# Two heads at a time in a dilated attention, and four more tiles for expert weights, in a two-block kernel on one core

## The chip, the core and the metric

The kernel runs on one core of a Trainium2 chip. The core has a matrix engine (PE in the profile, with its weight loads as PEld), a vector engine (DVE), an activation engine (ACT), a general engine (POOL) and a queue engine that issues transfers (SP). The metric is the device time of one execution in microseconds (us); smaller is better.

## What is computed

The program is a diffusion-style block of two layers, and then a second block of another kind, on 256 tokens of width 1024, batch 1, all in float32. The change lies in the second block alone, whose reference is, cut to what matters:

```python
def dilated_branch(q, k, v, window, dilation):   # query i sees keys i + j*dilation, |j| <= window // (2*dilation)
    ...
    s = jnp.where(valid, q @ k.T * 64 ** -0.5, -inf)
    m = max(s); p = exp(s - m); return p @ v, m, sum(p)
...
for window, dilation in ((128, 1), (512, 4), (2048, 16)):      # 12 heads of 64
    num, den, m = merged over the three branches
...
def second_block(x, mem, ...):
    u = rms_norm_2(x) @ w_in                                   # conv part, q, k, v
    c = conformer_conv(u[..., :512], ...)                      # gate, 31 depthwise taps, layer norm, silu
    a = dilated_attention(q, k, v, positions)
    x = x + concatenate([rms(c), rms(a)]) @ w_out
    x = x + memory_cross_attention(rms(x), rms(mem), ...)
    x = x + hierarchical_moe(rms(x), ...)                      # 32 experts, 2 per token
```

The kernel merges the three branches into one softmax: where a key is seen by n branches, 8 ln n is added to its score before the scale 1/8, and -1e30 where it is seen by none. This table of 256 by 256 is called the mask here.

## The kernel before

All weights are stored in HBM and are read once, in pieces of 128 partitions by 1024 float32 values (512 KB). They and most activations live in one pool of equal tiles in the on-chip memory, `u`, each 4 KB per partition; its size is `NSLOT`, 42 tiles. A transfer into a new tile must wait until the tile that had the place before is no longer read. Small work tiles are `t`, `s`; PSUM tiles are `ps`, eight banks.

Most matrix products use three passes in the fast rounding format fp32r: a weight piece is split by ACT (the high part, `u<-u 128x1024`) and by DVE (the rest, `TENSOR_TENSOR u<-u 128x1024`), then 24 matmuls of 256 columns follow on PE for each piece. Plain float32 matmuls take two records each in the trace.

The order of the work is planned when the program is built. Generators (one for the projections, one for the attention, one for the convolution, ...) yield the data that they wait for next; `drive` steps the one whose data will be there first by a small planner's clock (`Timer`), and pulls a filler, here the values of the later memory attention (weights `w_xv`), when all would wait. The engines then run their queues strictly in that order. `PACE` spaces out the 31 taps of the conformer's convolution, which are VectorE work: tap t is let go when the planner's PE clock has advanced by PACE times (t + 1) us.

The second block runs in these stages, with their place in the trace. From 1354 to 1475 us: the projections (`projections2`, weights w_in), the conformer's convolution (`conformer`) and the dilated attention (`dilated_attention`). From 1475 us: the product with w_out (`project_mix`), whose first matmuls read the conformer's output, the tile pair called Mc here, and then the attention's. From 1512 to 1566 us: memory attention, with weights w_xq and w_xo. Then the routing, and from 1595 us the 32 experts (`moe`), 384 pieces of weights.

Expert pieces are asked for ahead: `pump(n)` issues transfers until n pieces are waiting, and `AHEAD` holds n for six places: the memory attention's queries, the two parts of w_xo, the start of the experts, and two places within them. One piece after the other stands in SP's queue, between the weights of the stage that runs. When the first expert product starts, tiles are held by the pieces, by four tiles of the hidden state, two of the one-hot routing and one scratch tile; three pieces lie in other tiles (`tab`, `t`).

In the attention before, one head is done at a time. Its scores are two plain float32 matmuls that contract over 64 rows, half of the array; behind each, two fp32r matmuls with the identity (`identr`) add the high and the low part of the mask in PSUM. `softmax_pair` takes the maximum on DVE out of PSUM, the exponential on ACT, and the division. `turn_probs` transposes, and two matmuls with 64 output rows give the head's output.

Of the kernel before, what the change touches and what calls it, by code (L numbers as in the profile page):

```python
# [12 lines left out]
F32R = mybir.dt.float32r  # L13
# [3 lines left out]
OP = mybir.AluOpType  # L17
# [13 lines left out]
NSLOT = 42  # L31
# [387 lines left out]
class Net:  # L419
# [3 lines left out]
    PACE = 1.5  # L423
# [8 lines left out]
    AHEAD = (6, 16, 27, 34, 27, 28)  # L432
# [1085 lines left out]
    def start_second(self):  # L1518
# [11 lines left out]
        self.identr = self.cp.tile([128, 128], F32R, name="identr")  # L1530
        nc.scalar.activation(self.identr, self.ident, AF.Copy)
# [69 lines left out]
    def rotary_tables(self):  # L1601
# [6 lines left out]
        ln = self.tmp().rearrange("p (i k) -> p i k", i=2)  # L1608
        nc.gpsimd.dma_start(ln, self.a["lnmult"])
        ang, n, r = (self.tmp()[:, :SEQ] for _ in range(3))  # L1610
        yield (pos, ln)
# [11 lines left out]
        self.mask = Part(self.u([128, 2, 2, SEQ], F32R))  # L1623
        self.divide([(self.mask[:, 0], self.mask[:, 1], ln)], [self.mask])
# [52 lines left out]
    def softmax_pair(self, ps, scale):  # L1677
# [3 lines left out]
        P = Part(self.tmps(SEQ)[0])  # L1681
        nc.vector.tensor_reduce(m, ps, axis=AX, op=OP.max)
# [74 lines left out]
    def dilated_attention(self, Q, K, V, A, then):  # L1757

        nc = self.nc
        P, PT, turned = {}, {}, self.pairs(SEQ)  # L1760
        for hd in range(HEADS2 + 3):
            if hd < HEADS2:
                c, rows = hd // 2, slice(64 * (hd % 2), 64 * (hd % 2) + 64)
                while len(K) <= c:
                    yield BLOCK
                yield from self.until(Q[c], K[c], self.mask)
# [9 lines left out]
            if 0 <= hd - 2 < HEADS2:  # L1776
                yield from self.until(P[hd - 2])
                PT[hd - 2] = self.turn_probs(P.pop(hd - 2), next(turned))
            if hd >= 3:
                g = hd - 3  # L1780
                while len(V) <= g // 4:
                    yield BLOCK
# [620 lines left out]
```

## Time and profile before

| | us |
|---|---|
| median of 3 runs | 2062.21 (2062.17 to 2062.32) |
| the profiled execution | 2062.49 |
| its span in the trace | 2060.7 |
| PE busy over the span | 1935.8 (94%) |
| DVE busy over the span | 1085.6 (53%) |
| ACT busy over the span | 715.9 (35%) |
| expert weights, 384 pieces | 201.3 MB of 432.1 MB |

Shares over the whole span mix stages with different limits, so the stretches are read apart. A busy PE is not PE at its peak, since starts and ends of matmuls overlap: what a matmul costs in a queue is the distance between starts. Times in the rows are counted from the start of the span.

### The profile page before, as it was taken

What the parts mean: (1) busy time and instruction counts of PE and PEld (TensorE: products, weight loads), DVE (VectorE), ACT (ScalarE), POOL (GpSimd) and SP (SyncE); (2) the same over time, 40 slices, a digit from 0 to 9 for tenths busy, and PEclk for the clock granted to TensorE, in tenths of its full rate; (3) what the DMA queues carried; (4) which work ended last, traced back from release to release, by engine and by line L of the source; (5) the groups of instructions that cost most, each with busy time, mean ns of one, the idle gap of its engine ahead of it and who ended that gap; (6) DMA issues with size and microseconds to landing.
All of it is one profiled execution on the core that took longest, in us unless ns stands there. A gap on an engine that the chain in (4) does not pass through costs nothing. (4 is left out here: it accounts for less than half of the span.)

```text
span 2060.7 us, 28054 instructions
## 1 busy us (share of the span) xinstructions
PE 1935.8 (94%) x11179; PEld 1449.0 (70%) x11179; DVE 1085.6 (53%) x1759; ACT 715.9 (35%) x1170; POOL 41.2 (2%) x49
## 2 busy tenths in 40 slices
PE   7999999998999999999999999999999888888886
PEld 3788777886878888899889999998899421111111
DVE  6988888256863333598878655577664210000001
ACT  3433664233332222364654444446652100000001
POOL 0000000000000000000000000000000000000000
PEclk9999999998999999999999999999999999999998
DMA  9533235333543332545267455543269999999997
GB/s 368 168 101 122 67 97 184 124 121 112 169 136 103 92 114 72 166 162 190 68 244 263 158 183 185 176 141 113 92 198 340 395 409 409 409 409 409 409 409 299
DMA packets 121438, 432.11 MB, mean 210 GB/s; under 512 B 13654, under 2 KB 14152, under 8 KB 121304
## 3 DMA queue, kind: packets, MB, share of 16 engines
q1 hardware_dynamic: 119464, 424.64, 57.6%
q0 software_dynamic: 1696, 5.38, 0.9%
q8 instruction: 89, 1.46, 0.3%
q14 instruction: 45, 0.37, 0.1%
q10 hardware_dynamic: 144, 0.26, 0.0%
HBM read 428.13 MB, written 2.10 MB: 209 GB/s over the span
## 5 line engine op out<-in xcount | busy, mean ns | idle before, releaser
L289 PE MATMUL ps<-u 128*128 128x256 f32 (+2 forms) x9088 | 1599.5, 345 | 51.1 <-DVE u L289 24.6
L289 PEld LDWEIGHTS ps<-u 128*128 128x128 f32 (+1 forms) x9088 | 1294.5, 186 | 342.2 <-DMA u<-w 105.8
L289 DVE TENSOR_TENSOR u<-u 128x1024 fp32r<-128x1024 f32 (+4 forms) x414 | 432.6, 1071 | 205.5 <-ACT u L289 166.7
L289 ACT ACTIVATE u<-u 128x1024 fp32r<-128x1024 f32 (+3 forms) x392 | 360.4, 960 | 281.1 <-DVE u L289 224.8
L289 PE MATMUL ps<-u,t 128*32 128x512 f32 (+1 forms) x1028 | 216.9, 620 | 36.0 <-DMA u<-w 21.2
L289 PEld LDWEIGHTS ps<-u,t 128*32 128x32 f32 (+1 forms) x1028 | 44.2, 112 | 192.9 <-DMA u<-w 116.4
L289 ACT ACTIVATE u<-ps 128x512 f32<-128x512 f32 (+3 forms) x207 | 92.2, 487 | 226.9 <-PE ps L289 223.7
L289 DVE TENSOR_TENSOR t<-t,ps 128x512 f32<-128x512 f32 x12 | 8.2, 685 | 259.8 <-PE ps L289 259.8
L289 DVE SCALAR_TENSOR_TENSOR u<-u,cs 128x1024 f32<-128x1024 f32 x112 | 140.1, 1278 | 0.8 <-DMA u<-w_mod 0.7
L289 ACT ACTIVATE t<-ps 128x512 f32<-128x512 f32 (+1 forms) x62 | 36.2, 594 | 266.3 <-PE ps L289 266.2
L289 DVE TENSOR_TENSOR u<-u,ps 128x512 f32<-128x512 f32 x53 | 36.1, 686 | 105.6 <-PE ps L289 105.6
L289 DVE SCALAR_TENSOR_TENSOR u<-ps,mod,u 128x256 f32<-128x256 f32 x96 | 41.9, 479 | 83.4 <-PE ps L289 83.3
L289 DVE SCALAR_TENSOR_TENSOR u<-ps,s,u 128x512 fp32r<-128x512 f32 (+2 forms) x24 | 15.4, 662 | 118.1 <-ACT u L289 98.3
L289 DVE TENSOR_TENSOR u<-ps,u 128x128 fp32r<-128x128 f32 (+2 forms) x135 | 59.9, 490 | 29.2 <-ACT u L289 22.9
L289 ACT ACTIVATE u<-t 128x512 fp32r<-128x512 f32 (+1 forms) x74 | 41.6, 591 | 85.3 <-DVE t L289 76.7
L289 ACT ACTIVATE u<-ps,s 128x512 fp32r<-128x512 f32 (+1 forms) x26 | 15.8, 640 | 154.4 <-PE ps L289 150.8
L289 ACT ACTIVATE t<-ps,s 128x256 f32<-128x256 f32 (+1 forms) x80 | 49.2, 623 | 46.6 <-DVE s L289 45.8
L289 POOL TENSOR_TENSOR s<-s,mhalf 128x4 f32<-128x4 f32 (+2 forms) x25 | 30.0, 1200 | 1676.1 <-DVE s L289 1676.1
L289 PE MATMUL ps<-ident,t 128*128 128x128 f32 (+1 forms) x352 | 49.0, 273 | 7.4 <-DVE t L289 7.3
L289 ACT ACTIVATE t<-u 128x512 f32<-128x512 f32 x41 | 25.3, 628 | 84.9 <-DVE u L289 84.7
L289 PEld LDWEIGHTS ps<-ident,t 128*128 128x128 f32 (+1 forms) x352 | 39.7, 140 | 19.4 <-DVE t L289 14.9
L289 DVE TENSOR_REDUCE s<-ps 128x1 f32<-128x512 f32 (+2 forms) x65 | 38.4, 617 | 17.1 <-PE ps L289 16.9
(130 smaller groups left out, 705.2 us busy)
## 6 DMA issues: line engine op xcount, KB each, us to landing
u<-w SPq DMA_DIRECT2D x381, 512.0 KB, 10.2
u<-w_in SPq DMA_DIRECT2D x102, 512.0 KB, 4.2
u<-w_mod SPq DMA_DIRECT2D x96, 512.0 KB, 4.5
u<-w_gu SPq DMA_DIRECT2D x88, 512.0 KB, 4.0
u<-w_dn SPq DMA_DIRECT2D x32, 512.0 KB, 3.6
u<-w_out SPq DMA_DIRECT2D x24, 512.0 KB, 4.3
u<-w_oa SPq DMA_DIRECT2D x16, 512.0 KB, 4.6
u<-w_dn SPq DMA_DIRECT2D x16, 384.0 KB, 3.2
```

Of the source, the lines that this page charges most:

```text
L289: return fn(*args, **kw)
```

## The change

Six edits, of which the first three belong together.

1. `dilated_attention` takes a pair of heads at a time. The scores of the two heads use rows 0 to 63 and 64 to 127 of the array, in turn, into two PSUM banks; the two heads' outputs go to the two halves of the columns of one bank, in turn, and are copied out together.
2. The two matmuls per score that added the mask are gone, with the identity and the split mask that they read. `softmax_pair` adds the mask on DVE instead, out of PSUM into a work tile, which the maximum and the exponential then read.
3. The transposes of a pair come one step after its scores, where a head's came two steps after.
4. `PACE` goes from 1.5 to 2.2.
5. `NSLOT` goes from 42 to 46, and the six numbers of `AHEAD` go up by 3 or 4.
6. The scratch that POOL's transfers use for their descriptors is set to 2048 bytes per partition, from a default of 16384; the four tiles take the room.

```diff
-NSLOT = 42
+NSLOT = 46
...
-    PACE = 1.5
+    PACE = 2.2
...
-    AHEAD = (6, 16, 27, 34, 27, 28)
+    AHEAD = (9, 19, 30, 38, 31, 32)
...
-        self.identr = self.cp.tile([128, 128], F32R, name="identr")
-        nc.scalar.activation(self.identr, self.ident, AF.Copy)
...
-        ln = self.tmp().rearrange("p (i k) -> p i k", i=2)
-        nc.gpsimd.dma_start(ln, self.a["lnmult"])
+        self.mask = self.u([128, 2, SEQ])
+        nc.gpsimd.dma_start(self.mask, self.a["lnmult"])
...
-        self.mask = Part(self.u([128, 2, 2, SEQ], F32R))
-        self.divide([(self.mask[:, 0], self.mask[:, 1], ln)], [self.mask])
...
-    def softmax_pair(self, ps, scale):
+    def softmax_pair(self, ps, scale, add=None):
...
+        if add is not None:
+            nc.vector.tensor_tensor(P.ap, ps, add, op=OP.add)
+            ps = P.ap
...
-        for hd in range(HEADS2 + 3):
+        n = HEADS2 // 2
+        for c in range(n + 2):
...
-                ps = self.ps().rearrange("p (i k) -> p i k", i=2)
+                ps = [self.ps().rearrange("p (i k) -> p i k", i=2) for _ in range(2)]
                 for i in range(2):
-                    q = slice(i * 128, (i + 1) * 128)
-                    nc.tensor.matmul(ps[:, i], Q[c][rows, q], K[c][rows], start=True, stop=False,
-                                     skip_group_check=True)
-                    for part in range(2):
-                        nc.tensor.matmul(ps[:, i], self.identr, self.mask[:, part, i], start=False, stop=part == 1,
-                                         skip_group_check=True)
-                P[hd] = self.softmax_pair(ps, 0.125)
+                    for hh in range(2):
+                        rows = slice(64 * hh, 64 * hh + 64)
+                        nc.tensor.matmul(ps[hh][:, i], Q[c][rows, i * 128:(i + 1) * 128], K[c][rows], start=True,
+                                         stop=True, skip_group_check=True)
+                P[c] = [self.softmax_pair(p, 0.125, self.mask) for p in ps]
...
                 for k in range(2):
-                    nc.tensor.matmul(ps[:64], v[:, k, cs], pt[:, k], start=k == 0, stop=k == 1)
-                rows = slice(64 * (g % 2), 64 * (g % 2) + 64)
-                nc.scalar.activation(A[g // 4][rows, g // 2 % 2], ps[:64], AF.Copy)
+                    for hh in range(2):
+                        c0 = 64 * (2 * (g % 2) + hh)
+                        nc.tensor.matmul(ps[64 * hh:64 * hh + 64], v[:, k, c0:c0 + 64], pt[hh][:, k], start=k == 0,
+                                         stop=k == 1, skip_group_check=True)
+                nc.scalar.activation(A[g // 2][:, g % 2], ps, AF.Copy)
...
-    nc = bacc.Bacc("TRN2", target_bir_lowering=False, num_devices=1)
+    nc = bacc.Bacc("TRN2", target_bir_lowering=False, num_devices=1, dynamic_dma_scratch_size=2048)
```

PE before, in the middle of the attention, around the scores of the fifth and the sixth head; `u_12811` and `u_12579` hold Q and K, `identr_103` the identity, `64x256` is a head's output:

```order
L289 MATMUL ps_12877<-u_12811,u_12579 128x256
L289 MATMUL ps_12877<-u_4373,identr_103 128x256 x2
L289 MATMUL ps_12877<-u_12811,u_12579 128x256
L289 MATMUL ps_12877<-u_4373,identr_103 128x256 x2
L289 MATMUL ps_12900<-ident_76,t_12540 128x128 x4
L289 MATMUL ps_12906<-u_12602,u_12579 64x256 x2
L289 MATMUL ps_12912<-u_12811,u_12579 128x256
```

PE now, at the scores of the same two heads (third pair of six):

```order
L289 MATMUL ps_12901<-u_12780,u_12491 128x256
L289 MATMUL ps_12902<-u_12780,u_12491 128x256
L289 MATMUL ps_12901<-u_12780,u_12491 128x256
L289 MATMUL ps_12902<-u_12780,u_12491 128x256
L289 MATMUL ps_12933<-ident_76,t_12550 128x128 x4
L289 MATMUL ps_12939<-ident_76,t_12560 128x128 x4
L289 MATMUL ps_12945<-u_12659,u_12491 64x256 x4
```

Four score matmuls of two heads now stand together, with no matmul of the mask between them, and the four output matmuls of an earlier pair stand together too.

DVE now, from the splits of weights behind which that pair's softmax stands to the rotation of the next queries (`t<-ps,u` is the new addition of the mask, the SCALAR_TENSOR_TENSOR rows with `cols` are convolution taps, two per tap):

```order
L289 TENSOR_TENSOR u<-u 128x1024 x3
L289 TENSOR_TENSOR t<-ps,u 128x512
L289 TENSOR_REDUCE s<-t 128x2
L289 TENSOR_SCALAR s<-s 128x2
L289 TENSOR_TENSOR t<-ps,u 128x512
L289 TENSOR_REDUCE s<-t 128x2
L289 TENSOR_SCALAR s<-s 128x2
L289 RECIPROCAL s<-s 128x2
L289 SCALAR_TENSOR_TENSOR t<-u,cols,t 128x256 x4
```

Where one head's maximum stood alone between taps, two heads' additions and maxima now stand in a row, with taps still in the queue, which had run out before this point.

SP at the memory attention, as a piece of the difference; `u<-w` are expert pieces:

```order
 L289 DMA u<-w_xq 128x1024 x8
 L289 DMA u<-w 128x1024 x6
-L289 DMA u<-w_xo 128x1024 x8
+L289 DMA u<-w_xo 128x1024
+L289 DMA u<-w 128x1024 x3
+L289 DMA u<-w_xo 128x1024 x7
 L289 DMA u<-w 128x1024 x15
```

Three more expert pieces now stand ahead of seven of the eight pieces of w_xo.

## Rows read from the trace of the kernel before

**Rows 1.** Stretches: us, busy us of PE, PEld, DVE, ACT, POOL; clock, DMA share, GB/s.

```profile
1354.00:1474.00 120.00, 119.56 (x831) 101.08 (x830) 89.92 (x181) 70.46 (x150) 1.39 (x2) 1.00 0.32 106
...
1595.00:2044.00 449.00, 384.75 (x1777) 98.40 (x1778) 37.21 (x72) 23.23 (x41) 0.58 (x1) 0.98 1.02 405
```

**Rows 2.** Timeline of PE, attention: start, us, what, count of records [idle before].

```profile
1379.46 0.70 PE L289 MATMUL ps<-u 64*128 64x256 f32 x2
1380.08 0.50 PE L289 MATMUL ps<-u,identr 128*128 128x256 f32 x2
1380.51 0.70 PE L289 MATMUL ps<-u 64*128 64x256 f32 x2
...
1468.38 1.08 PE L289 MATMUL ps<-u 128*64 128x256 f32 x4
```

**Rows 3.** Timeline of PE, the first expert product.

```profile
1595.33 3.64 PE L289 MATMUL ps<-u,t 128*32 128x512 f32 x32 [0.58 <-DVE t L289]
```

**Rows 4.** Groups by shape, 1340 to 1505 us: an addition out of PSUM on DVE (us, mean ns).

```profile
L289 DVE TENSOR_TENSOR u<-ps,u 128x512 fp32r<-128x512 f32 x2 | 1.4, 684 | 0.0
```

**Rows 5.** Timeline of DVE in the attention's stretch.

```profile
1361.51 0.69 DVE L289 TENSOR_TENSOR t<-ps,tab 128x512 f32<-128x512 f32 x1 [5.38 <-PE ps L289]
...
1364.35 0.74 DVE L289 TENSOR_SCALAR t<-u,cols 128x256 f32<-128x256 f32 x2
...
1367.74 0.74 DVE L289 STREAM_SHUFFLE t<-ps 128x512 f32<-128x512 f32 x1
...
1370.28 2.46 DVE L289 SCALAR_TENSOR_TENSOR t<-u,cols,t 128x256 f32<-128x256 f32 x6
1372.65 1.22 DVE L289 TENSOR_TENSOR u<-u 128x1024 fp32r<-128x1024 f32 x1
...
1381.79 0.69 DVE L289 TENSOR_REDUCE s<-ps 128x2 f32<-128x512 f32 x1
...
1382.58 0.87 DVE L289 SCALAR_TENSOR_TENSOR t<-u,cols,t 128x256 f32<-128x256 f32 x2
```

**Rows 6.** Timeline of DVE: the conformer's layer norm begins; Mc is finished.

```profile
1423.09 0.69 DVE L289 TENSOR_REDUCE s<-ps 128x2 f32<-128x512 f32 x1 [2.10 <-PE ps L289]
...
1456.19 0.69 DVE L289 TENSOR_TENSOR u<-t,u 128x512 fp32r<-128x512 f32 x1 [1.26 <-ACT u L289]
```

**Rows 7.** Timeline of PE: last head's output, then 36 matmuls with w_out.

```profile
1473.75 5.54 PE L289 MATMUL ps<-u 128*64 128x256 f32 x40
```

**Rows 8.** Timeline of PE, then a stretch as in rows 1, at its end.

```profile
1504.60 1.86 PE L289 MATMUL ps<-ones,t 128*128 128x1 f32 x8 [2.17 <-ACT t L289]
1506.33 5.38 PE L289 MATMUL ps<-u 128*128 128x256 f32 x24
...
1500.00:1510.00 10.00, 7.83 (x46) 7.62 (x46) 8.28 (x15) 5.29 (x8) 2.55 (x5) 0.73 0.90 273
```

**Rows 9.** Timeline of SP: expert pieces (`w`), first issue, us to the last, count.

```profile
1502.46 20.35 SPq L289 DMA_DIRECT2D u<-w  x6
...
1541.71 23.20 SPq L289 DMA_DIRECT2D u<-w  x15
1564.96 0.93 SPq L289 DMA_DIRECT2D tab<-w  x2
...
1568.65 21.15 SPq L289 DMA_DIRECT2D u<-w  x14
...
1597.27 42.66 SPq L289 DMA_DIRECT2D u<-w  x38
```

**Rows 10.** A stretch as in rows 1: where the experts start.

```profile
1590.00:1600.00 10.00, 8.35 (x68) 4.81 (x67) 6.03 (x19) 0.47 (x1) 0.00 (x0) 1.00 0.65 233
```

**Rows 11.** Waits from 1354 to 1480 us: us in total, times, longest.

```profile
DVE s L289 <- PE ps L289: 12.0, 7, 2.7
DVE t L289 <- PE ps L289: 11.1, 4, 5.4
```

**Rows 12.** Transfers issued by POOL: count, KB each, median us to landing.

```profile
stash<-u POOLq DMA_DIRECT2D x4, 256.0 KB, 7.2
```

More of the change, by code (lines that the diff above doesn't have):

```diff
@@ L1760, in dilated_attention @@
         P, PT, turned = {}, {}, self.pairs(SEQ)
-        for hd in range(HEADS2 + 3):
-            if hd < HEADS2:
-                c, rows = hd // 2, slice(64 * (hd % 2), 64 * (hd % 2) + 64)
+        n = HEADS2 // 2
+        for c in range(n + 2):
+            if c < n:
                 while len(K) <= c:
                     yield BLOCK
-                yield from self.until(Q[c], K[c], self.mask)
-                ps = self.ps().rearrange("p (i k) -> p i k", i=2)
+                yield from self.until(Q[c], K[c])
+                ps = [self.ps().rearrange("p (i k) -> p i k", i=2) for _ in range(2)]
@@ L1776, in dilated_attention @@
[L1776 to L1781, printed above, removed]
+                    for hh in range(2):
+                        rows = slice(64 * hh, 64 * hh + 64)
+                        nc.tensor.matmul(ps[hh][:, i], Q[c][rows, i * 128:(i + 1) * 128], K[c][rows], start=True,
+                                         stop=True, skip_group_check=True)
@@ L1782, in dilated_attention @@
+                P[c] = [self.softmax_pair(p, 0.125, self.mask) for p in ps]
+                del ps
+            if 0 <= c - 1 < n:
+                yield from self.until(*P[c - 1])
+                PT[c - 1] = [self.turn_probs(p, next(turned)) for p in P.pop(c - 1)]
+            if c >= 2:
+                g = c - 2
+                while len(V) <= g // 2:
                     yield BLOCK
-                yield from self.until(V[g // 4], PT[g])
+                yield from self.until(V[g // 2], *PT[g])
@@ L1784, in dilated_attention @@
                 pt = PT.pop(g)
-                v = V[g // 4]
+                v = V[g // 2]
                 ps = self.ps()[:, :SEQ]
-                cs = slice(64 * (g % 4), 64 * (g % 4) + 64)
                 for k in range(2):
-                    nc.tensor.matmul(ps[:64], v[:, k, cs], pt[:, k], start=k == 0, stop=k == 1)
-                rows = slice(64 * (g % 2), 64 * (g % 2) + 64)
-                nc.scalar.activation(A[g // 4][rows, g // 2 % 2], ps[:64], AF.Copy)
-                if g % 4 == 3:
-                    then(g // 4)
+                    for hh in range(2):
+                        c0 = 64 * (2 * (g % 2) + hh)
+                        nc.tensor.matmul(ps[64 * hh:64 * hh + 64], v[:, k, c0:c0 + 64], pt[hh][:, k], start=k == 0,
+                                         stop=k == 1, skip_group_check=True)
@@ L1795, in conformer @@
+                nc.scalar.activation(A[g // 2][:, g % 2], ps, AF.Copy)
+                del ps
+                if g % 2:
+                    then(g // 2)
     def conformer(self, C, out):
```

2 lines of the change are left out of this document (1 added, 1 removed).

## The prediction, made before the changed kernel ran

> **What bounds the kernel now.** I read the stretches first, then the queues inside them. In the attention's stretch PE is busy 119.56 of 120 us at a granted clock of 1.00, DVE 89.92, and the DMA share is 0.32 [rows 1]: matmuls set the time, and DVE has 30 us left. From the experts' start at 1595 to 2044 the DMA share is 1.02 at 405 GB/s [rows 1]: there transfers set the time, 449 x 405 = 181.8 MB, or 347 pieces of 524 KB at 1.295 us each. So the change can gain in two ways: less PE time before the experts, or fewer pieces still to load when they start. DVE's waits [rows 11] tell what slack it has today: 23.1 us in waits for PSUM results.
>
> **Scores and outputs on halves (PE).** A half of a head's scores starts at 1379.46, its mask at 1380.08, the next half at 1380.51 [rows 2]: 0.62 + 0.43 = 1.05 us, four times for a pair, 4.2. The mask's 0.43 goes. Of the 0.62, streaming is about 0.45: sixteen float32 matmuls of 512 columns on quarters of the array take 3.64 [rows 3], 0.228 each with four side by side, so 0.91 for one alone and 0.45 for 256 columns; the other 0.17 is changing over. Two halves side by side: 2 x 0.45 + 0.15 = 1.05 a pair. Outputs: four records in 1.08, starts 0.25 apart [rows 2], so 1.0 a head and 2.0 a pair; side by side 1.0. Six pairs give 6 x (3.2 + 1.0) = 25 us. That column quarters overlap, rows 3 show (0.228 against 0.5 for half the columns); that row halves do no row shows, so its bounds are both halves overlapping (25) and neither (4 x 0.45 + 0.1 = 1.9 a pair and outputs unchanged: 14). I take 25, since the pieces of rows 3 are the nearest.
>
> The Trainium skill ("TensorEngine Tiling (Array Packing)", Theoretical Speedup and Gotcha 1) puts row halves at up to twice the speed if they write different PSUM banks, as they do here. No row of before shows it.
>
> **The mask on DVE.** Twelve additions out of PSUM. The same shape has a mean of 684 ns [rows 4]; by starts, less the overhang of some 0.08, 0.60. So 7.2 to 8.2 us more for DVE. Whether this costs nothing depends on where DVE stands, which I count through its queue. Prices, each a duration less about 0.08: a tap (two instructions, 0.87, or 2.46 for three) 0.395 per instruction, a split 1.14 [rows 5]; a rotation of queries or keys 2.54 (three 512-wide products and a shuffle at 0.6 to 0.66 each [rows 5]); a head's softmax 0.60 for the addition and 0.79 for maximum and scale (1381.79 to 1382.58 [rows 5]), 1.40; a division's reciprocal 0.08.
>
> From the first tap, 1364.35 [rows 5], to the end of the fifth pair's key rotation the changed order holds on DVE 54 tap instructions (21.3), 14 splits (16.0), 6 rotations (15.2), eight heads (11.2) and small ones (1.2): 64.9, so 1429.2, and 1431.5 with the waits for PE that I find in the order on the way. PE has up to the same place 444 matmuls of 0.122 (36 in 5.54 less 1.00 for the outputs ahead and an overhang [rows 7]; 54.0), nine groups of transposes (4.0), four pairs of scores (4.2) and two of outputs (2.0): from 1361.4, where DVE's long wait ends [rows 5], that is 64.2, or 1425.6. **So DVE, not PE, is now last there**, by about 6 us, which PE waits. Wider-spread taps are the reason: they stand among the softmaxes.
>
> From there to the first matmul with w_out PE has scores 2.1, transposes 5.0, outputs 4.0, 120 matmuls 14.6, sums with ones and their spreads 4.6: 30.3. Waits in it: for the last taps and the conformer's transposes 2.3, the last pair's softmax 1.3, the conformer's sums 1.6 (each a DVE or ACT step with nothing else ready on PE in the order): 5.5 with small ones. So w_out starts at 1431.5 + 30.3 + 5.5 = 1467.3. Before, it starts at 1473.75 + 1.00 = 1474.75 [rows 7]: 7.4 earlier. As fillers, 24 matmuls with w_xv (2.9), twelve sums and two spreads (3.0), which stood behind that point, now stand ahead of it: 5.9 more. Together 13.3 of the 25; without any wait w_out would start at 1455.9 and all 25 would be kept, which checks the count (1474.75 - 25 + 5.9 = 1455.7).
>
> New waits may also lower the clock. In 1500 to 1510 the granted clock is 0.73, that is partly at 1.2 instead of 2.4 GHz; PE had waited 2.17 for ACT, and the 24 matmuls behind took 5.38 instead of 2.9 [rows 8]: 2.4 for one such fall. I charge one: **11 us** kept.
>
> **Four more tiles, earlier asking.** Before, 6 + 15 + 1 + 2 + 14 = 38 pieces are issued before the first freed tile lets the next go at 1597.27 [rows 9] (the issue pair at 1564.96 is half-size, and with its likes makes three pieces in other tiles); after, 42. Every piece that is there when the experts start shortens their transfers by 1.295: 4 x 1.295 = 5.2. They need room earlier: three stand ahead of w_xo, behind the six issued from 1502.46 on, and 1590 to 1600 has a DMA share of 0.65 [rows 10], 3.5 us unused. Against this the whole span ahead of the experts is shorter, so the fewer idle DMA microseconds cost 0.7: **4.5**. Below: nothing, if SP's queue, in which w_xo's pieces now stand behind three expert pieces (3 x 1.295 = 3.9 later at worst), delays memory attention by as much as the tiles give. At the top 5.2.
>
> **The rest.** A smaller descriptor scratch moves no byte. POOL's four stash transfers take 7.2 to land [rows 12]; if the smaller ring makes POOL stand until one has landed, the routing's small steps behind the last of them on POOL could be up to 7.2 late. A gain is not excluded either (the same transfers from less room), but no row shows POOL waiting for the ring; I take 0 and keep 0 to 7.2. The identity's copy, the mask's split and its load are off the path before the second block; the copies of outputs on ACT become half as many, in a stretch where ACT has 70.46 of 120 [rows 1]. Hidden, and of no cost if they weren't (under 1 us). That transposes follow after one step instead of two shows as the waits above.
>
> **The sum.** 2062.49 (the profiled execution) - 11 - 4.5 = 2047.0; the median is 0.3 below the profiled one, so **2046.7**. About 0.2% (4 us) is what a measurement of this kernel can tell from no change.
>
> **The rivals.**
>
> 1. *PE stays the bound.* DVE starts ahead of its queue and the additions fit the slack of 23.1 [rows 11]; then 25 and 5.2 come in full: 2062.2 - 30 = 2032. For it: 30 us of DVE's stretch are idle. Against: my count of its queue. 0.12.
>
> 2. *Halves don't run side by side.* 11 us of PE's 25 are not there. The waits of 6 us at the fifth pair go first (PE itself is there at 1425.6 + 5.4 = 1431), the other 5.7, behind it, count: 2046.7 + 5 = 2051.7. 0.10.
>
> 3. *The clock falls more often.* With w_out at 1467 and some five waits ahead of it, each may be followed by a slow stretch at 2.4 [rows 8]. Three instead of one: 2046.7 + 4.8 = 2051.5. 0.08. The Trainium skill says as much ("TensorE: Matmul & The Clock Gate", HAM oscillation): gaps between bursts of matmuls can hold the clock at half. Rows 8 agree, with 0.73 behind a gap of 2.17.
>
> 4. *The pieces bring nothing,* since what goes earlier delays w_xo: 2046.7 + 4.5 = 2051.2. 0.05.
>
> 5. *Only the tiles count:* waits for DVE eat all that PE saves: 2062.2 - 4.5 = 2057.7, within what can be told from no change or just beyond. 0.08, which I count as no change.
>
> 6. *Slower: the conformer ends too late.* DVE has its 64.9 us without slack, and taps are spread until 1441 in my count. If it still must wait 23.1 for PE's results as now [rows 11], because it stands in strict order, the last tap comes near 1462.5. From the layer norm's first sum to Mc's low part 33.8 us pass now (1423.09 to 1456.19 + 0.69 [rows 6]), with other work between; then Mc is there at 1496.3, and w_out's first matmuls read it: 21.5 later than 1474.75, less 5.9 moved ahead and 4.5 of tiles: 2062.2 + 11 = 2073. It decides for slower by over 0.2% from Mc at 1489 on, that is 16 of the 23.1. Against it: a third of the chain is other work that would then be done already, and w_xv's matmuls fill. 0.06.
>
> 7. *The change doesn't do what it says:* the ring's size makes POOL wait for a whole landing, 7.2 [rows 12], on top of the forecast: 2053.9. 0.02; nothing in the trace speaks for it.
>
> **How the numbers follow.** The forecast itself has 0.49, with a range of its own from 2040 (DVE gets 6 us ahead of my count) to 2054 (7 more of its waits for PE stay). Faster: 0.49 + 0.12 + 0.10 + 0.08 + 0.05 + 0.02 = 0.86; same 0.08; slower 0.06. For the range, slower and most of the tail of rival 5 stay out above (2058 holds its centre), and below it reaches to rival 1 at 2032: about 0.8 with the tails of both.
>
> **What will show it.** A pair's scores: four matmuls with starts adding up to near 1.05 us, outputs near 1.0; nearer 1.9 and 2.0 is rival 2. DVE between 1361 and 1440 busy nearly throughout, and PE's idle time ended by DVE: rival 1 has neither. The first w_out matmul near 1467, the experts' first about 13 before 1595, granted clock below 1.00 in at most one more stretch. 42 pieces issued before the first freed tile, and the DMA share in the experts still at 1.0. POOL with no wait ahead of its routing step. Wrong would be: PE's idle time in the stretch under 5 or over 20, Mc behind the last output by more than 5 us, or experts that start earlier while the end doesn't move as much.

## The result and the profile after

The changed kernel takes 2039.74 us (median of four, 2037.84 to 2041.31) against 2062.27 for the kernel before beside it: 0.9881 of its time, 95% interval 0.9863 to 0.9900. That is 22.5 us less, inside the range from 2032 to 2058, and 7 below the forecast of 2046.7. But the traces tell that the sum came out near for a wrong reason: most of the gain lies in the program's first layers (the first block here: all up to 1346 us of the kernel before), of which the prediction does not speak at all.

The profiled execution of after took 2037.84, its span 2036.0. Four marks that both kernels have show where the 24.7 us between the spans (2060.72 and 2036.04) went. The marks are the last sum with `mod` on DVE, which ends the first block; the sums of squares behind w_out (`ones,acc`); the first expert product; the end.

| mark | before, us | after, us | gain up to here | gain since the mark above |
|---|---|---|---|---|
| first block ends | 1346.20 | 1329.76 | 16.4 | 16.4 |
| sums behind w_out | 1500.66 | 1482.39 | 18.3 | 1.8 |
| first expert product | 1595.33 | 1574.89 | 20.4 | 2.2 |
| end | 2060.72 | 2036.04 | 24.7 | 4.2 |

So the attention's own stretch, for which I had 7 to 13 us, gained 1.8, with the time to the experts 4.0. Between the first mark and the third both traces hold the same number of matmuls of 128 by 256 (1395 and 1394 records), but not between the first and the second: ahead of the sums behind w_out the changed kernel does 24 matmuls of the memory attention's values (w_xv) more, some 2.9 us at 0.122 each. All the following times of after are 16.4 us earlier on the way to the attention, and have to be read with that shift.

PE in the first block before, in the timeline (start, us, what, count of records, idle time before):

```profile
251.07 3.21 PE L289 MATMUL ps<-u 128*128 128x512 f32 x13
257.22 4.90 PE L289 MATMUL ps<-u 128*128 128x512 f32 x23 [2.94 <-DVE u L289]
...
298.58 1.54 PE L289 MATMUL ps<-u 128*128 128x512 f32 x5 [2.13 <-DVE u L289]
```

The same matmuls after:

```profile
250.46 7.77 PE L289 MATMUL ps<-u 128*128 128x512 f32 x36
```

Thirteen matmuls, a wait of 2.94 for DVE, 23 more; after, all 36 in one run. PE's idle time between 240 and 350 us was 7.2 (102.82 busy of 110), after 0.3 (109.66 of 110), and where it had waited its clock had fallen too (0.91 in 295 to 315). The same matmuls stand 3.7 us earlier at 257.22 of the kernel before, 10.3 at 315.85, 12.8 at 607.77 and 16.3 at 1039.95. Over the whole first block PE idles 36.2 us instead of 46.2 and is busy 1293.6 instead of 1300.0: 10.0 of the 16.4 are waits that are gone. The other 6.4 are shorter busy time for as many matmuls; its cause is told only in part by the clock, whose mean is 0.99 in both.

PE of after at the attention (the first row is the fifth pair's scores, the third begins with the rest of the sixth pair's, the fourth is the fourth pair's outputs):

```profile
1414.51 1.13 PE L289 MATMUL ps<-u 64*128 64x256 f32 x8 [1.57 <-DVE u L289]
1415.57 1.09 PE L289 MATMUL ps<-ident,t 128*128 128x128 f32 x8
...
1419.66 5.74 PE L289 MATMUL ps<-u 64*128 64x256 f32 x30 [1.35 <-DVE t L289]
...
1428.08 1.08 PE L289 MATMUL ps<-u 128*64 128x256 f32 x8
1429.09 1.87 PE L289 MATMUL ps<-ident,t 128*128 128x128 f32 x12
...
1437.82 1.67 PE L289 MATMUL ps<-u 128*128 128x256 f32 x12
1445.14 1.87 PE L289 MATMUL ps<-ones,t 128*128 128x1 f32 x8 [5.65 <-ACT t L289]
...
1453.06 2.91 PE L289 MATMUL ps<-u 128*128 128x256 f32 x12
```

Eight records, four matmuls, of scores take 1.13 us for a pair and 1.06 to the next start (1415.57), where a pair had taken 4.2 [rows 2]; outputs 1.08, to the next start (1429.09) 1.01, where they had taken 2.0 [rows 2]. The halves do run side by side, at the price that was predicted. But PE then waits: 1.57 and 1.35 for DVE, and 5.65 for ACT at the conformer's sums, behind which PE is slow up to 1457: twelve matmuls took 1.67 at 1437.82 and 2.91 at 1453.06.

Stretches of after (us, busy us of PE, PEld, DVE, ACT, POOL; clock, DMA share, GB/s):

```profile
1355.00:1414.00 59.00, 55.72 (x445) 51.15 (x444) 58.02 (x118) 36.13 (x80) 0.00 (x0) 1.00 0.37 115
1414.51:1459.60 45.09, 38.01 (x244) 33.34 (x245) 29.80 (x60) 28.80 (x64) 2.76 (x4) 0.81 0.23 73
1445.00:1459.00 14.00, 13.86 (x71) 13.86 (x72) 4.32 (x9) 4.44 (x10) 2.06 (x3) 0.55 0.04 11
```

From the end of the first block to the sums behind w_out, before and after, in the same columns:

```profile
1346.20:1500.66 154.46, 153.57 (x1111) 134.43 (x1110) 113.35 (x221) 87.55 (x178) 6.34 (x9) 1.00 0.34 113
1329.76:1482.39 152.63, 141.76 (x1091) 132.55 (x1090) 121.04 (x234) 85.84 (x173) 6.80 (x11) 0.94 0.38 118
```

PE is busy 11.8 us less, with those 24 matmuls more, and idles 10.0 us more (10.87 instead of 0.89); its clock was 1.00 and is 0.94.

Up to the fifth pair DVE is busy 58.02 of 59 us: it is now the engine that ends last, where PE had been [rows 1]. Behind the wait of 5.65 the granted clock is 0.55, the lower of the two levels (1.2 instead of 2.4 GHz) for nearly all of 14 us. The Trainium skill ("TensorE: Matmul & The Clock Gate", HAM oscillation) says that gaps between bursts of matmuls can hold the clock at half; this stretch agrees, with 0.55 behind 5.65 of idling.

What ACT did in those 5.65 us:

```profile
1436.21 3.92 ACT L289 ACTIVATE u<-u 128x1024 fp32r<-128x1024 f32 x4
...
1440.47 1.09 ACT L289 ACTIVATE u<-u 128x1024 fp32r<-128x1024 f32 x1
...
1442.11 1.28 ACT L289 ACT_TABLE_LOAD   x1
1443.41 1.02 ACT L289 ACTIVATE t<-ps,cols 128x256 f32<-128x256 f32 x2
1444.46 0.63 ACT L289 ACTIVATE t<-t 128x512 f32<-128x512 f32 x1
```

The conformer's silu and square (1443.41, 1444.46), which PE waits for, stand behind five splits of weights and a table load. Mc, which w_out's first matmuls read, is finished on DVE only at 1457.07 + 0.69:

```profile
1457.07 0.69 DVE L289 TENSOR_TENSOR u<-t,u 128x512 fp32r<-128x512 f32 x1 [0.69 <-ACT u L289]
```

Before, the conformer's end fell among the heads' matmuls [rows 6], with other work for PE.

At the next gap, behind w_out, in after:

```profile
1486.33 1.05 PE L289 MATMUL ps<-ones,t 128*128 128x1 f32 x8 [2.17 <-ACT t L289]
1487.25 23.34 PE L289 MATMUL ps<-u 128*128 128x256 f32 x180
...
1574.89 4.64 PE L289 MATMUL ps<-u,t 128*32 128x512 f32 x32 [0.58 <-DVE t L289]
```

The same gap of 2.17 as in [rows 8]. The ten microseconds from the sums behind it, before and after, in the columns of the stretches:

```profile
1504.60:1514.60 10.00, 10.00 (x58) 10.00 (x59) 6.89 (x12) 4.71 (x7) 1.55 (x1) 0.66 0.70 256
1486.30:1496.30 10.00, 9.97 (x71) 9.97 (x72) 7.57 (x12) 3.62 (x5) 1.62 (x1) 0.83 0.94 306
```

The clock fell in both, for half as long after: 0.83 instead of 0.66, and 180 matmuls follow in 23.34, 0.130 each. It was low again in the first expert product, 4.64 instead of 3.64 [rows 3].

### The profile page after: what moved, and what is told of

It is laid out like the page before. It is cut to its first block, busy times and chain, and to the rows that moved or that the text cites. A ratio compares the mean times of both kernels' runs of the same rounds, so it can differ in the third digit from the quotient of the medians.

```text
span 2036.0 us, 27905 instructions
## 1 busy us (share of the span) xinstructions
PE 1914.4 (94%) x11131; PEld 1440.8 (71%) x11131; DVE 1088.6 (53%) x1770; ACT 710.2 (35%) x1162; POOL 40.6 (2%) x49
## 5 line engine op out<-in xcount | busy, mean ns | idle before, releaser
L289 PE MATMUL ps<-u 128*128 128x256 f32 (+2 forms) x9088 | 1583.6, 346 | 49.8 <-DVE u L289 21.9
L289 PE MATMUL ps<-u,t 128*32 128x512 f32 (+1 forms) x1028 | 218.2, 616 | 30.3 <-DMA u<-w 21.4
L289 ACT ACTIVATE u<-ps 128x512 f32<-128x512 f32 (+3 forms) x201 | 88.1, 491 | 247.2 <-PE ps L289 246.9
L289 DVE TENSOR_TENSOR u<-u,ps 128x512 f32<-128x512 f32 x53 | 36.2, 685 | 109.3 <-PE ps L289 109.3
L289 DVE TENSOR_TENSOR u<-ps,u 128x128 fp32r<-128x128 f32 (+2 forms) x135 | 59.2, 488 | 22.8 <-ACT u L289 16.6
L289 PEld LDWEIGHTS ps<-ident,t 128*128 128x128 f32 (+1 forms) x352 | 39.8, 141 | 22.5 <-DVE t L289 14.7
L289 PE MATMUL ps<-ones,t 128*128 128x1 f32 x240 | 33.3, 264 | 14.2 <-ACT t L289 14.2
L289 ACT ACTIVATE t<-ps,s 128x512 f32<-128x512 f32 (+1 forms) x56 | 38.0, 688 | 23.0 <-DVE s L289 19.4
```

Source lines behind the costliest of these rows:

```text
L289: return fn(*args, **kw)
```

## The experiments

Theory A says that the tiles gave the first block's gain as well as the experts'; B is the prediction's view (attention 11, tiles 4.5); C puts the first block's gain down to the smaller descriptor ring. Theories D and E (of what holds the attention back), F (of AHEAD) and G come with the later groups. In each group the runs shared one chip and their own runs of the kernel before. The medians of before were 2065.17, 2066.09, 2064.49 and 2063.88 in the four groups, and its single runs on one chip reached from 2060.5 to 2069.7; so differences between two changed kernels under some 3 us are not told apart by medians alone, and I use the marks of the traces there. A trace is one execution: with 46 tiles the first block's gain alone reaches from 15.3 to 18.0 in the traces below. The column to the sums behind w_out doesn't hold the same work in every kernel, since the planner moves matmuls with w_xv across that mark; where it matters I add it to the next column, the gain up to the experts.

### Which part gave the time: four kernels

`tiles_alone`:

```diff
-NSLOT = 42
+NSLOT = 46
...
-    AHEAD = (6, 16, 27, 34, 27, 28)
+    AHEAD = (9, 19, 30, 38, 31, 32)
...
-    nc = bacc.Bacc("TRN2", target_bir_lowering=False, num_devices=1)
+    nc = bacc.Bacc("TRN2", target_bir_lowering=False, num_devices=1, dynamic_dma_scratch_size=2048)
```

> The kernel before with 46 tiles, the larger AHEAD numbers and the 2 KB descriptor scratch; its attention is unchanged. Theory A (in the changed kernel 16.4 us were already gained at 1340 us of the kernel before, ahead of the attention; the four tiles gave them, because weights of the first block came late when no tile was free, and gave 4.3 more in the experts): 2062.3 - 16.4 - 4.3 = 2041.6, 2039 to 2045, with the first 1340 us shorter by 16. Theory B (my prediction: tiles count only in the experts): 2062.3 - 4.5 = 2057.8.

`attention_alone` (of the changed kernel, the three edits above taken back):

> The changed kernel with 42 tiles, the old AHEAD and the default scratch: heads in pairs, mask on DVE, PACE 2.2 alone. Theory A: only what lies between 1354 us and the experts, 20.4 - 16.4 = 4.0, so 2058.3, and nothing ahead of 1340 us. Theory B: 11 us, 2051.

`tiles_old_ahead` (of the kernel before):

```diff
-NSLOT = 42
+NSLOT = 46
...
-    nc = bacc.Bacc("TRN2", target_bir_lowering=False, num_devices=1)
+    nc = bacc.Bacc("TRN2", target_bir_lowering=False, num_devices=1, dynamic_dma_scratch_size=2048)
```

> The kernel before with 46 tiles and the 2 KB scratch, but the old AHEAD. Theory A: the first block's 16.4 us in full, and no more expert pieces ahead: about 2046, the experts' own stretch as long as before. Theory B: 2062, since it holds that more tiles without earlier asking are of no use.

`ring_alone` (the second of these two edits alone):

> The kernel before with the 2 KB descriptor scratch alone, 42 tiles. Theory A and B: 2062.3, no change. Rival C (what was gained ahead of 1340 us is the smaller ring's doing, through POOL's transfers in the first block): 2046, with the first 1340 us shorter by 16.

| kernel | median, us | ratio to before (interval) | gain in the first block | to the sums behind w_out | to the experts | in the experts |
|---|---|---|---|---|---|---|
| changed | 2039.74 | 0.9881 (0.9863 to 0.9900) | 16.4 | 1.8 | 2.2 | 4.2 |
| tiles_alone | 2044.84 | 0.9900 (0.9878 to 0.9922) | 15.3 | 0.0 | -1.5 | 3.6 |
| attention_alone | 2066.16 | 0.9997 (0.9983 to 1.0012) | -2.2 | 1.8 | 0.4 | -3.4 |
| tiles_old_ahead | 2040.96 | 0.9882 (0.9861 to 0.9903) | 16.8 | -0.9 | 0.0 | 4.9 |
| ring_alone | 2064.03 | 0.9997 (0.9984 to 1.0010) | -2.3 | 0.0 | 0.0 | -0.2 |

Theory A holds: with 46 tiles the first block is 15 to 17 us shorter, with 42 it isn't, whatever else is changed (the -2.2 and -2.3 are alike, though only one of the two has the small ring; neither edit explains them). The ring has no effect: rival C falls. And the attention by itself is worth nothing that can be measured: theory A gave it 4.0, and it has 2.2 up to the experts and loses 3.4 in them; its first product ran at a lower clock there (5.34 instead of 3.64), which is 1.7 of the 3.4.

`tiles_old_ahead` is a surprise beside this: it keeps the whole gain, 4.9 in the experts included, with the old AHEAD. In its trace 45 issues of expert weights stand ahead of the first expert product, as many as in the changed kernel and four more than before (41; three pieces are issued in halves). `after_old_ahead`, below, has 45 as well. So the number of pieces ahead goes with the tiles and not with AHEAD. That `tiles_alone` is 3.9 us slower would be a price of the larger numbers if it came back elsewhere; two other runs below speak against that.

### How many tiles: 44

```diff
-NSLOT = 42
+NSLOT = 44
...
-    nc = bacc.Bacc("TRN2", target_bir_lowering=False, num_devices=1)
+    nc = bacc.Bacc("TRN2", target_bir_lowering=False, num_devices=1, dynamic_dma_scratch_size=2048)
```

> The kernel before with 44 tiles, the 2 KB scratch and the old AHEAD. Theory A with a price for each tile (weights come as much earlier as there is room): half of what 46 tiles gave, 2053, with 6 to 10 us gained ahead of 1340 us. Rival (a threshold: one certain weight must fit): all of it, 2041, or nothing, 2063.

2045.19 us, 0.9909 (0.9893 to 0.9926). The first block gains 16.0 with two tiles, 16.8 with four: the rival's threshold, not a price for each tile. In the experts two tiles give 2.4 and four, with the same AHEAD, 4.9, as if each tile counted there; but other kernels with 46 tiles have 1.3 to 4.2 in the experts, so one trace each doesn't show it. What happened in the first block, in SP's timeline (issue, us, what; `w_in` is a weight of the first block, this its second piece here). Before:

```profile
246.38 0.33 SPq L289 DMA_DIRECT2D u<-w_in  x1
```

With 44 tiles:

```profile
235.58 0.33 SPq L289 DMA_DIRECT2D u<-w_in  x1
```

It was issued 10.8 us earlier, and PE's 2.94 us of waiting at 257.22 are gone:

```profile
249.61 7.81 PE L289 MATMUL ps<-u 128*128 128x512 f32 x36
```

What that wait ended with is not a step on the weight. Before, on DVE, a split of a weight and then, behind one more scaling, the step that PE waited for, the low part of a result out of PSUM:

```profile
254.14 1.23 DVE L289 TENSOR_TENSOR u<-u 128x1024 fp32r<-128x1024 f32 x1 [1.72 <-issue]
...
256.48 1.28 DVE L289 TENSOR_TENSOR u<-ps,u 128x512 fp32r<-128x512 f32 x2
```

It stands late because of what is ahead of it in DVE's order. The weight is one such thing. Another is ACT, which writes the rounded results of PSUM into tiles of the same pool; before, and then with 44 tiles:

```profile
242.57 0.58 ACT L289 ACTIVATE u<-ps 128x512 fp32r<-128x512 f32 x1
246.16 0.60 ACT L289 ACTIVATE u<-ps 128x512 fp32r<-128x512 f32 x1 [3.02 <-PE ps L289]
```

```profile
241.12 1.06 ACT L289 ACTIVATE u<-ps 128x512 fp32r<-128x512 f32 x2
```

With 44 tiles both are written in one go; with 42 the second waits 3.02 for PE, and DVE's steps behind it wait too. I read this as a wait for a tile that PE still reads. So the missing tiles hold up weights and results; no run separates the two.

SP's queue waits are a place to look at before a run. From 0 to 1340 us of the kernel before (engine and line, what it waits for: us in total, times, longest):

```profile
SPq L289 <- PE ps L289: 751.3, 200, 24.9
```

and PE in the same stretch:

```profile
PE ps L289 <- DVE u L289: 24.9, 17, 4.8
```

SP waits more than half of the time for PE, the reader of a tile, and that total hardly changes (after: 724.9). PE's waits tell more: after, and with 44 tiles, 17.8 and 18.0 us in 11 waits. The six that are gone are five that ended with the low part of a result (2.94, 2.13, 0.23, 0.22, 0.88) and one that ended with the scaling of a weight (1.59). The five that ended with the split of a whole weight piece, 1.19 to 2.35 each, are all still there. A step into a tile that comes late and PE waiting behind it are one chain, and I had looked for it only in the second block.

### What holds the attention back: taps, additions, order of halves

`pace_15` (of the changed kernel):

```diff
-    PACE = 2.2
+    PACE = 1.5
```

> The changed kernel with PACE back at 1.5. Theory D (the wider taps end the conformer late, so that PE waits 5.65 us for ACT at 1439.5 and then runs at half clock to 1459, some 6 us more; both would go): the conformer's sums now stand in the order ahead of the fifth pair's scores, the wait and the half clock at that place go, some 4 to 5 us of waits for the last pair's softmax come instead: 2035, 2032 to 2038. Rival E (DVE has the same work in another order and stays last): 2040, with PE's idle time in the stretch the same in sum.

`no_add` (of the changed kernel; it leaves the mask out, so its attention sees every key; the routing then differs, and what lies behind it isn't comparable):

```diff
-                P[c] = [self.softmax_pair(p, 0.125, self.mask) for p in ps]
+                P[c] = [self.softmax_pair(p, 0.125) for p in ps]
```

> The changed kernel without the addition of the mask, so the attention is computed unmasked: twelve additions of 0.60 to 0.72 us are left out on DVE, nothing else. Theory D (DVE is last up to the fifth pair's scores): these start 5 to 6 us earlier and the time falls by as much or somewhat more with the shorter wait behind: 2034, 2031 to 2037. Rival E2 (the conformer's end on ACT sets the start of w_out, whatever DVE does): 2039 to 2041.

`after_old_ahead` (of the changed kernel):

```diff
-    AHEAD = (9, 19, 30, 38, 31, 32)
+    AHEAD = (6, 16, 27, 34, 27, 28)
```

> The changed kernel with the old AHEAD numbers on its 46 tiles. Theory F (three expert pieces ahead of w_xo hold up memory attention, as the run of the tiles with the old numbers, 3.9 faster than with the new, suggests): 2036, 2034 to 2039. My prediction's term (four more pieces at the experts' start are worth 4.5): 2044.

`halves_in_row` (of the changed kernel; the same exchange of the two loops, there k and hh, at the outputs):

```diff
-                for i in range(2):
-                    for hh in range(2):
+                for hh in range(2):
+                    for i in range(2):
```

> The changed kernel with the four score matmuls and the four output matmuls of a pair ordered head by head, so that the two halves of the array alternate once instead of three times. If only neighbours on different halves overlap: scores 3 x 0.45 + 0.15 = 1.5 us a pair instead of 1.05, outputs 1.75 instead of 1.0, 7 us more PE time in all; the time 2 to 5 us longer, 2042 to 2045, if PE's time counts, and 2040 if DVE is last. If the halves overlap by themselves in any order: 1.05 and 1.0 as before, and 2040.

| kernel | median, us | ratio to before (interval) | first block | to the sums behind w_out | to the experts | in the experts |
|---|---|---|---|---|---|---|
| pace_15 | 2037.69 | 0.9863 (0.9841 to 0.9886) | 17.4 | 0.4 | 3.4 | 4.2 |
| no_add | (3830.96) | | 17.6 | 7.0 | 1.4 | |
| after_old_ahead | 2040.54 | 0.9876 (0.9856 to 0.9897) | 16.8 | 1.4 | -0.3 | 1.3 |
| halves_in_row | 2038.80 | 0.9871 (0.9850 to 0.9892) | 18.0 | 1.9 | 2.2 | 2.8 |

The median of `pace_15` lies in theory D's 2032 to 2038, but its trace speaks for rival E. PE in its stretch:

```profile
1399.82 1.13 PE L289 MATMUL ps<-u 64*128 64x256 f32 x8 [1.45 <-DVE u L289]
...
1427.60 0.95 PE L289 MATMUL ps<-ones,t 128*128 128x1 f32 x8
...
1447.59 0.66 PE L289 MATMUL ps<-ident,t 128*128 128x128 f32 x4 [1.63 <-ACT t L289]
```

The conformer's sums (1427.60) now come without a wait, and the 5.65 us are gone; but the third pair's scores wait for DVE at 1399.82, transposes wait 1.63 for ACT at 1447.59, and more such waits lie between. PE idles 9.4 of 120 us, in the changed kernel 10.9 (1344 to 1464). The sums behind w_out come only 0.4 us earlier than before, with 60 matmuls of w_xv more ahead of them (the changed kernel: 24). Up to the experts the gain is 3.8, the changed kernel's 4.0. The wider spacing of the taps is neither a gain nor the loss: it moves the waits from one place to another.

`no_add` shows the shortage itself. At its sums behind w_out (1476.12) 7.0 us are gained instead of 1.8, with the same 24 matmuls ahead: 5.1 for the 7.2 us that twelve additions take at 0.60. The stretch from the first block's end, as for after above:

```profile
1328.61:1476.12 147.51, 137.97 (x1092) 128.68 (x1091) 113.43 (x222) 83.92 (x173) 8.40 (x11) 0.98 0.38 123
```

PE idles 9.54 instead of 10.87 and is busy 137.97 instead of 141.76 with the same work, at a clock of 0.98 instead of 0.94. So only 1.3 of the 5.1 are waits that went; 3.8 go with the clock. Theory D holds in that the additions cost the path some 5 us. Its sign fails: the fifth pair's scores start at 1418.04 and not 5 to 6 us before 1414.51, in an order that the planner made anew. E2 falls: the conformer's sums, at 1441.92 instead of 1445.14, come earlier with a wait of 3.13 instead of 5.65.

`after_old_ahead` is within 1 us of the changed kernel's median, though on another chip (0.9876 and 0.9881 of before), neither 2036 (theory F) nor 2044 (my term). With the other pair, in which the old numbers were faster by 3.9, the larger AHEAD shows no effect of one sign.

`halves_in_row` gave the scores and the outputs of a pair in

```profile
1412.91 1.14 PE L289 MATMUL ps<-u 64*128 64x256 f32 x8 [1.56 <-DVE u L289]
...
1424.93 1.09 PE L289 MATMUL ps<-u 128*64 128x256 f32 x8
```

1.14 and 1.09, as with halves in turn (1.13 and 1.08). Two matmuls of one half in a row don't keep the other half's waiting: the 1.5 and 1.75 were wrong, and which of the two orders is written makes no difference.

### The mask on PE again, for pairs

`pair_mask_pe` (of the changed kernel with PACE 1.5; the identity and the split of the mask are put back):

```diff
-                P[c] = [self.softmax_pair(p, 0.125, self.mask) for p in ps]
+                for hh in range(2):
+                    for i in range(2):
+                        for part in range(2):
+                            nc.tensor.matmul(ps[hh][:, i], self.identr, self.mask[:, part, i], start=False,
+                                             stop=part == 1, skip_group_check=True)
+                P[c] = [self.softmax_pair(p, 0.125) for p in ps]
```

> The changed kernel with the mask added again by PE (eight matmuls with the identity per pair, behind the four scores) instead of DVE, and PACE 1.5. Theory D (DVE's additions are on the path, since without them the sums behind w_out came 6.3 us earlier): the gain of 6.3 comes back, less what of the 6 x 1.06 = 6.4 us of PE time isn't covered by the 9.4 us that PE idles in the run with PACE 1.5: 2034, 2031 to 2037. Rival G (PE's time counts in full once DVE is relieved): 2038 to 2041, no better than the changed kernel.

`pair_mask_pe_late` (the same with `AHEAD = (6, 16, 27, 38, 31, 32)`):

> The same with the first three AHEAD numbers back at 6, 16, 27, the others as in the changed kernel: no expert piece more ahead of w_xo, as many at the experts' start. If three pieces ahead of w_xo hold up memory attention: 2 us below the run beside it. If they don't: within 1 us of it.

In both, with all score matmuls of a pair ahead of the mask's, the attention's values differ from those of the kernel before; why, no run isolates. With another routing the whole times (3832.95 and 3834.89) can't be compared. The stretch before the routing does the same instructions as a right one would. The gains to the sums behind w_out are 4.4 and 4.2, between the changed kernel's 1.8 and the 7.0 without the mask. (The 6.3 of the expectation counts 1.2 of the first block; it is 5.1.) DVE is relieved and PE pays: a pair's eight mask matmuls take 1.05 us by starts (1363.47 to 1364.52), 6.3 for six, and PE still waits 3.26 for DVE at the fourth pair:

```profile
1363.47 1.21 PE L289 MATMUL ps<-u,identr 128*128 128x256 f32 x8
1364.52 3.04 PE L289 MATMUL ps<-u 128*128 128x256 f32 x24
...
1399.26 2.07 PE L289 MATMUL ps<-u 64*128 64x256 f32 x6 [3.26 <-DVE t L289]
```

But no matmul of w_xv was moved ahead of the sums here, and up to the experts the gain stays 4.4 and 4.2, where the changed kernel has 4.0. So moving the mask back gives next to nothing, not 6: rival G holds. The two AHEADs are 0.2 apart up to the experts, which again speaks against theory F.

### The addition and the maximum in one instruction

`fused_max` (of the changed kernel, with PACE 1.5):

```diff
         if add is not None:
-            nc.vector.tensor_tensor(P.ap, ps, add, op=OP.add)
+            for i in range(2):
+                nc.vector.tensor_tensor_reduce(P[:, i], ps[:, i], add[:, i], 1.0, -3.0e38, op0=OP.add, op1=OP.max,
+                                               accum_out=m[:, i:i + 1])
             ps = P.ap
-        nc.vector.tensor_reduce(m, ps, axis=AX, op=OP.max)
+        else:
+            nc.vector.tensor_reduce(m, ps, axis=AX, op=OP.max)
```

> The changed kernel with PACE 1.5, and the addition of the mask and the maximum done by one DVE instruction for each half of a head (two of 256 columns in place of an addition and a maximum of 512 each). No trace shows this instruction's time; the bounds are as long as both it replaces (1.32 us a head for the two) and as long as a maximum alone (0.69 for the two). Theory D (DVE's additions are on the path): at the lower bound 12 x 0.63 = 7.6 us of DVE go and some 6 of them reach the end as without the additions: 2032 against 2037.7; at the upper bound 2038. Rival G (relieving DVE brings PE's own time to the fore): not under 2036.

2028.60 us (five runs, 2027.30 to 2035.26), 0.9836 of before (0.9819 to 0.9853): its median is 11 us under the changed kernel's, 9 by the ratios (0.9836 and 0.9881), since the two ran on different chips, and 3 under the 2032 that theory D gave at the lower bound. Against `pace_15`, which differs in this one edit, it is 5.6 by the ratios (0.9863). It is faster than both kernels. DVE's timeline for a head in the changed kernel:

```profile
1397.30 0.68 DVE L289 TENSOR_TENSOR t<-ps,u 128x512 f32<-128x512 f32 x1
1398.02 0.69 DVE L289 TENSOR_REDUCE s<-t 128x2 f32<-128x512 f32 x1
1398.74 0.17 DVE L289 TENSOR_SCALAR s<-s 128x2 f32<-128x2 f32 x1
1398.81 0.68 DVE L289 TENSOR_TENSOR t<-ps,u 128x512 f32<-128x512 f32 x1
```

and here:

```profile
1397.54 0.42 DVE L289 CUSTOM_DVE_ANT_0 t<-ps,u 128x256 f32<-128x256 f32 x1
...
1397.88 0.42 DVE L289 CUSTOM_DVE_ANT_0 t<-ps,u 128x256 f32<-128x256 f32 x1
...
1398.35 0.17 DVE L289 TENSOR_SCALAR s<-s 128x2 f32<-128x2 f32 x1
1398.42 0.42 DVE L289 CUSTOM_DVE_ANT_0 t<-ps,u 128x256 f32<-128x256 f32 x1
```

A head takes 1.51 there (1397.30 to 1398.81) and 0.88 here (1397.54 to 1398.42): 0.63 less, 7.6 for twelve, as at the lower bound. The stretch from the first block's end, as above, and the first expert product:

```profile
1329.05:1475.37 146.32, 140.63 (x1115) 130.60 (x1114) 114.63 (x258) 86.36 (x174) 9.91 (x11) 0.99 0.42 130
```

```profile
1566.23 3.64 PE L289 MATMUL ps<-u,t 128*32 128x512 f32 x32 [0.58 <-DVE t L289]
```

PE idles 5.7 us instead of 10.9, its clock is 0.99 (in the changed kernel 0.94), and the first expert product runs in 3.64 instead of 4.64. The gains by mark: 17.2 in the first block, 8.1 to the sums behind w_out, 3.8 to the experts, 3.2 in them. Against `pace_15` the 7.6 less on DVE moved the experts' start by 8.1 (11.9 - 3.8), more than the 6 that theory D let through; PE idles 3.7 less than there (9.44), and its clock is 0.99 instead of 0.97. With 11.9 up to the experts, this kernel has the gain that I had forecast for the change itself. It was run with PACE 1.5 alone; how it would stand with 2.2 wasn't tried.

## Why the prediction was near, and where it was wrong

**The forecast held by two errors of opposite sign.** It charged 11 to the attention and 4.5 to the tiles; measured are 4.0 and 4.2, and 16.4 that it did not have.

1. *The tiles in the first block: the term that was missing.* I had priced the tiles at the one place that the edit's other half, AHEAD, names, the experts' start. But the pool serves the whole program. "Below: nothing ... At the top 5.2" was therefore no bound of the change. `tiles_old_ahead` alone is worth 24.2 us (2065.17 to 2040.96), as much as the whole change.

2. *The tiles in the experts: near in size, the cause not borne out.* 4.2 against 4.5. With the old AHEAD the traces give 4.9 and 1.3, and 45 issues stand ahead of the experts just the same: the earlier asking is not what brings them there. That w_xo might be delayed by three pieces (rival 4) shows with neither sign: from the sums to the experts the larger numbers are 1.5 worse with the old attention, 2.5 better with the new and equal in the last pair of runs.

3. *Scores and outputs on halves: right.* 1.06 and 1.01 for a pair, predicted 1.05 and 1.0. Of the bounds 14 and 25 the upper one holds; rival 2 falls. That PE saves so much and gains so little is told by points 4 and 5.

4. *DVE becomes the last up to the fifth pair: right.* The count of its queue gave 1431.5 for the fifth pair's scores; with the 16.4 of the first block that is 1415.1, and they start at 1414.51, with DVE busy 58.02 of 59 us up to there. Rival 1 falls: the slack of 23.1 [rows 11] was no room for 8 us more. In the same stretch of after (1338 to 1464) DVE still waits 15.3 for PE, 9.7 of it behind the conformer's sums; that the slack lay where it was of no use is my reading of this.

5. *From there to w_out: the step that failed.* Predicted 30.3 of work and 5.5 of waits, 35.8; measured 45.1, from 1414.51 to 1459.6 (the first of the twelve matmuls with w_out that end the run of 36 at 1456.04). PE idles 7.1 of it (45.09 - 38.01), 1.6 more than predicted. It does so at other places: the conformer's sums wait 5.65 instead of 1.6, since ACT's queue (five splits, a table load) was not counted, while those for the last taps and the last pair's softmax did not come, and one of 1.35 at the sixth pair's scores did. The larger part is the clock. PE is busy 38.0 for the 30.3 of work, 7.7 more, at a granted clock of 0.81 over the stretch. **The mis-sized term is the clock: I charged 2.4 for one fall, and it took 7.7.** Between 1445 and 1459 the clock is 0.55, and twelve matmuls took 2.91 instead of 1.67; at these two durations the 13.86 busy us would have been some 8, so about 6 are that fall, an estimate from these rows. The rest lies behind the wait of 1.35 at the sixth pair (0.61 from 1419.66 to 1424). The 13.3 us of the prediction less 1.6 and 7.7 are 4.0; measured up to the experts are 4.0. Rival 3, more falls than one, has the right mechanism.

6. *Rival 6, the conformer too late,* came true in its place, not in its size: Mc is there at 1457.76, and w_out starts at 1459.6, which is 1476.0 on the clock of before, 1.3 behind the old 1474.75 where 7.4 ahead was forecast, but far from 1489. That the sums behind it still come 1.8 earlier is owed to the work that now stands ahead of w_out: from its start to them it takes 22.8 us (1459.6 to 1482.39) instead of 25.9. The 2.2 from the sums to the experts have the same source in part, since the 24 matmuls with w_xv, 2.9 us, no longer stand there; but `attention_alone`, with the same 24 moved, gains 0.4 there.

   *Rival 5, only the tiles count,* is nearest to the runs: `attention_alone` is 0.9997 of before, and `tiles_old_ahead`, without the new attention, 0.9882 where the whole change is 0.9881. What ate PE's saving was the clock as well as the waits, and the tiles' gain lay in the first block.

7. *The ring: right.* `ring_alone` is 0.9997 of before; rival 7 falls.

8. *What would show it.* "PE's idle time in the stretch under 5 or over 20" would not have caught the error: it is 10.9. "Mc behind the last output by more than 5 us" did: the last outputs start at 1436.38 and end by 1437.5, and Mc is there at 1457.76, 20 us later. So did "granted clock below 1.00 in at most one more stretch", and "experts about 13 before 1595": they start 20.4 earlier.

What stays open: why the experts' own stretch differs by up to 3 us among kernels with 46 tiles (gains of 1.3 to 4.9). Their first product takes 3.64 to 6.29 us, which goes with part of it; no run was made on that alone. Open too is why the first block's busy time is shorter, and how much of the first block's gain comes through weights and how much through results that found no tile.

## What to carry to other kernels

A resource that the whole program shares (a pool's size) has to be priced wherever something waits for it: look for an engine that waits for a step into a tile of the pool, and follow the order of that step's engine back to a weight that SP issued late or to a write that stood until a tile was read, in every stage and not only in the one that the edit names. When work leaves the engine that bounds a stage, count the queue of the engine that gets it up to the next place where the first one waits, and go on counting through every engine (here ACT) to the stage's end. Price the lower clock behind each wait beside the wait itself: here it cost more (7.7 us) than the waits that the count had missed (1.6). The forecast gain of 11 came only when the added work was taken off that engine again, by one instruction that adds and takes the maximum in one pass.

## What had not been expected of the hardware

- Going from 42 to 44 tiles gave 16.0 us of the first block, two more 0.8, which is within the spread of the traces: the pool's effect there has a step.
- A DVE instruction that adds out of PSUM and keeps the maximum took 0.42 us for 128 by 256 values, 0.34 from start to start. For a head, two of them took 0.81 to the next step (1397.54 to 1398.35), where an addition and a maximum of 512 took 1.44 (1397.30 to 1398.74).
- Four float32 matmuls on two halves of the array took the same time head by head as in turn (1.14 and 1.13 us for scores, 1.09 and 1.08 for outputs).
- After the same gap of 2.17 us and the same sums the clock was 0.66 over ten microseconds in the kernel before and 0.83 in the changed one.
- Leaving out twelve additions on DVE took 1.3 us of PE's waits and 3.8 us of its busy time for the same matmuls: the clock rose from 0.94 to 0.98.
